# A planned transformer layer: sixteen feed-forward pairs by seven products, six kept results split at once, conditioning sums planned later

## The chip, the cores and the metric

One NeuronCore of a Trainium2 chip runs the kernel. The metric is device microseconds (us) of one execution, median of three runs. TensorE is PE in the profile (its weight loads PEld), VectorE is DVE, ScalarE is ACT, GpSimd is POOL, SyncE is SP; SPq and POOLq are the queues that issue DMAs.

## What is computed

One decoder layer on a 512 x 1024 activation, in float32: a token mixer (attention with 8 heads and a state-space scan with 16 heads, one input and one output projection), then a convolutional gated feed-forward net. A vector c gives shift, scale and gate of both halves through a 1024 x 6144 matrix.

```python
mod = (c_act @ ada_w[i] + ada_b[i])[:, None, :]
sh1, sc1, g1, sh2, sc2, g2 = jnp.split(mod, 6, axis=-1)
h = x * (1.0 + sc1) + sh1
y = hybrid_mixer(h, ...)
x = layer_norm(DEEPNORM_ALPHA * x + (1.0 + g1) * y, ln1_g[i], ln1_b[i])
h = x * (1.0 + sc2) + sh2
y = conv_ffn(h, ...)            # u = causal_dwconv(h @ w_up); (silu(g) * val) @ w_down
x = layer_norm(DEEPNORM_ALPHA * x + (1.0 + g2) * y, ln2_g[i], ln2_b[i])
```

## The kernel before

**Precision.** Each float32 operand is split into a high part (ACT copies it to fp32r) and a low part (DVE subtracts), and every product is three matmuls (high x high, low x high, high x low). So each weight tile costs a load on SP, an ACT copy (`wh`, or half of `wq`) and a DVE subtraction (`wl`, or the other half of `wq`).

**Order of work.** The program is written as generators, one for each chain of work (loads, splits, products, attention of one head pair, and so on). A planner at the head of the file (`Order`) runs them against a table of costs and latencies: at every step it takes, among the heads of all generators, the instruction that can start first by its plan, and among those of one engine that can start within 0.2 us of it the one with the lowest priority number. What it emits is a fixed order for each engine; waits on the chip follow from data. `Region` (L44) holds when a tile's parts are written and read by plan, `try_alloc` (L145) hands out tiles from pools with quotas (`R.limit`), and `start` (L235) works out an instruction's earliest start: written data counts as there after the writer's latency (`LAT`, L231: 1.0 us for a load on SP). Every engine instruction is issued through one helper, L308, so profile rows go by tile names.

**Stages.** First c's shift and scale and the first products; then the input projection (`fm`, `tm`) with attention (`psS` scores, `pT` transposes, `pov`) and the scan beside it; then the output projection (`po`) and the first normalisation (`ln1`, `pt` transposes); then the up projection of the feed-forward net, the *up stage*; last its down projection (`dn`) and the second normalisation.

**Conditioning sums.** `ada_acc` (L1083) loads eight 128 x 1024 pieces of the matrix (tile `ad`, two at a time) and adds each, times a column of c, to `acc` on DVE. `ada_row` and `ada_cols` (L1107, L1120) do that three times during input and output projection, and `ada_last` (L1779) once more, its pieces by two.

**The up stage.** There are 22 pairs of output tiles (gate and value). A pair is done directly (2 tiles x 8 pieces x 3 = 48 matmuls of 512 columns), or, if in `SEVEN` (L694), by seven half-size products as in Strassen's scheme (`seven`, L1660; 7 x 4 x 3 = 84 matmuls of 256 columns, `sP`). Pairs 0 and 1 are done directly in two halves. A seven-product pair needs sums of weight quarters: two are made by accumulating DMAs on POOL (`sums_seven`, L720), two on DVE (`sw`), and seven tiles are split into `wq` (`split_seven`, L763); its products are put together by seven DVE additions of 256 columns (`seven_out`, L1692). Then `up_post` (L1358) does a three-tap convolution on ACT and DVE and multiplies gate by value. The split weights (`wh`/`wl` or `wq`) share a quota `w2` of 11 buffers.

**Kept results.** The product for the down projection must again be split into high and low parts (`mid`). For pairs below `NMID` (4) `up_post` does it at once, in two buffers each. The others are kept unsplit in one tile (`keep`), and the generator `keep` (L1388) splits them once the up stage's tiles are free (mark `fin`), at priority 1. `up_post` runs at priority 2. When kept results 12 to 15 are split, their tiles go to the normalised x, which is loaded back (`x_back`) and scaled on POOL (`row_loads`).

```python
        if j >= NMID:
            ...
            k = KEPT[j] = KEEP[j - j % n][:, j % n]
            yield V.tensor_mul(k, g, u)
            ...
        yield V.tensor_mul(g, g, u)
        mid = yield buf("b", [P, 2, SEQ], "mid", "mid", F32R)
        yield A.activation(mid[:, 0], g, AF.Copy)
        yield V.tensor_sub(mid[:, 1], g, mid[:, 0].bitcast(F32))
```

Of the kernel before, what the change touches and what calls it, by code (L numbers as in the profile page):

```python
# [43 lines left out]
class Region:  # L44


    def __init__(self, base=0.0):
        self.base, self.wr, self.rd, self.psum, self.whole = base, {}, {}, False, False

    def end(self):  # L50
        return max([self.base] + [v[0] for v in self.wr.values()] + [v[0] for v in self.rd.values()])
# [56 lines left out]
class Order:  # L108
# [37 lines left out]
    def try_alloc(self, a):  # L146
        if a.after:
            if self.due(a) > self.time:
                return None
            a.after = ()  # L150
        pool, slots = self.pools[a.cls]
        group = a.group or a.cls
        if self.used.get(group, 0) >= self.quota.get(group, 1000):
            return None
        free = [s for s in slots if s["free"]]
        if not free:
            return None
        s = min(free, key=lambda q: q["end"])
        t = pool.tile(a.shape, a.dt, name=self.name(a.name), tag=s["tag"], bufs=1)
        s["free"] = False  # L160
        self.used[group] = self.used.get(group, 0) + 1
        self.regs[t.tensor.name] = Region(s["end"])
        self.regs[t.tensor.name].psum = a.cls == "ps"
        self.regs[t.tensor.name].whole = a.name == "sP"
        self.owner[t.tensor.name] = (s, group)
        return t

# [71 lines left out]
    def start(self, op, margin=0.0):  # L239
        t = self.clock["G" if op.eng == "GD" else op.eng]  # L240
        for k in op.ins + (op.outs if op.eng == "GD" else []):
            if k:
                r = self.regs[k[0]]
                t = max(t, r.base)
                for c in k[1]:
                    w = r.wr.get(c)
                    assert w or k[0].startswith("dr"), ("read before write", op.fn, k[0], c)
                    if w and w[1] != op.eng:
                        t = max(t, w[0] + self.LAT[w[1]] + margin)
                    elif w:  # L250
                        t = max(t, w[0] + self.SAME[op.eng])
                if r.psum:
                    t = max([t] + [q[0] + 0.12 for q in r.rd.values() if q[1] != op.eng])
        for k in op.outs:
            if k:
                r = self.regs[k[0]]
                t = max(t, r.base)
                for c in k[1]:
                    for w in (r.wr.get(c), r.rd.get(c)):
                        if w and w[1] != op.eng:  # L260
                            t = max(t, w[0] + 0.09 + margin)
        if op.port:
            for a, b in self.held["G" if op.eng == "V" else "V"]:
                if a <= t < b:
                    t = b
        return t
# [146 lines left out]
def layer_kernel(  # L413
# [21 lines left out]
    R = Order(nc)  # L435
    T, V, A, G, S, GD = (Engine(R, k) for k in ("PE", "V", "A", "G", "S", "GD"))
# [26 lines left out]
    def buf(cls, shape, name, group=None, dt=F32):  # L463
        return Alloc(cls, shape, dt, name, group)
# [226 lines left out]
            rows_item(w_out, k, n)  # L691
    UP0 = len(items)
    NSPLIT = 4
    SEVEN = [3, 5, 6, 8, 9, 11, 12, 13, 15, 16, 17, 18, 19, 20, 21]  # L694
    for j, i in up_tiles:
        cols_item(w_up, i * D_FF + j * P)
    for n in range(2):
# [4 lines left out]
    def w_load():  # L702
        yield Need("loads")
        for i, (shape, src) in enumerate(items):
# [4 lines left out]
            j = (i - UP0) // 2  # L709
            if i == UP0 + 2 * j + 1 and j in SEVEN:  # L710
                R.spawn(sums_seven(j, raw, items[i - 1][1][:, :4], src[:, :4]), 4)
# [3 lines left out]
    def sums_seven(j, r1, a11, a21):  # L715

        q = yield buf("s", [P, 4, P], "sw")
        yield S.dma_start(q, a11)
        yield GD.dma_start(r1[:, :4], r1[:, 4:], accum_op=OP.add)
        yield GD.dma_start(q, a21, accum_op=OP.add)  # L720
        QS[j] = q
        R.mark(("qs", j))

    def w_split():
        yield Need(("hk", KC - 1))
        for i, (shape, _) in enumerate(items):
# [6 lines left out]
            if 0 <= i - len(items) + LATE_DN < 2:  # L733
                yield Need("fin")
                m = 2 * (i - len(items) + LATE_DN)
                hi, lo = RES["w"][:, m], RES["w"][:, m + 1]
            elif UP0 <= i < UP0 + 2 * NFF and (i - UP0) // 2 in SEVEN:
                if (i - UP0) % 2 == 0:
# [63 lines left out]
    def w_next():  # L802
        i = wpos[0]
        wpos[0] += 1
        if not (UP0 <= i < UP0 + 2 * NFF and (i - UP0) // 2 in SEVEN):
            lead[0] += 1
# [538 lines left out]


    MID, U, E8 = {}, {}, {}
    NMID = 4
    KEEP, KEPT = {}, {}

    def conv3(ps, dst, ch, neg):
# [6 lines left out]
    def up_post(j, i, ps, neg=False):  # L1358
# [8 lines left out]
        g = U.pop(j)  # L1367
        if j >= NMID:
            if not 12 <= j < 20 and j % 2 == 0:
# [18 lines left out]
    def keep():  # L1388

        yield Need("tsused")  # L1390
        for j in (12, 16):
            KEEP[j] = yield buf("e", [P, 4, SEQ], "keep")
            R.mark(("keep", j))
        yield Need("fin")
        for j in range(NMID, NFF):
            if 12 <= j < 20:
                if j % 2 == 0:
                    E8[j] = yield buf("e", [P, 2, 2, SEQ], "mid2", dt=F32R)
                mid = E8[j - j % 2][:, j % 2]
            else:  # L1400
                mid = yield buf("b", [P, 2, SEQ], "mid", "mid", F32R)
            yield Need(("kept", j))
            yield A.activation(mid[:, 0], KEPT[j], AF.Copy)
            yield V.tensor_sub(mid[:, 1], KEPT[j], mid[:, 0].bitcast(F32))
            MID[j] = mid
            R.mark(("mid", j))
            n = 4 if 12 <= j < 20 else 2
            if j % n == n - 1:
                R.free(KEEP[j - j % n])
                R.mark(("kfree", j - j % n))  # L1410
# [306 lines left out]
    def ffn():  # L1717
        h2h, h2l = H2["hl"]
        pend = []
        for part in range(2):  # L1720
            c0, c1 = part * 256, part * 256 + 256
            for j, i in up_tiles[:NSPLIT]:
                if part == 0:
                    key, n_ = w_next()
                    ps = yield bank("gemm", "up")
                    yield Need(key)
                    w = W.pop(n_)
                    pend.append((ps, w))
                else:
                    ps, w = pend.pop(0)  # L1730
                for k in range(KC):
                    yield Need(("h2", 2 * part, k // 4), ("h2", 2 * part + 1, k // 4))
                    yield mm3(ps[:, c0:c1], w[0][:, k], w[1][:, k], h2h[:, k, c0:c1], h2l[:, k, c0:c1],
                              k == 0, k == KC - 1)
                if part == 1:
                    R.free(*w)
                    R.spawn(up_post(j, i, ps), 2)
        R.free(ROWS.pop("g1p"))
        R.limit(raw=5, w2=11, gemm=8)
        for n, (j, i) in enumerate(up_tiles[NSPLIT:]):  # L1740
            if j in SEVEN:
                if i == 0:
                    yield from seven(j)
                continue
            key, n_ = w_next()
            ps = yield bank("gemm", "up")
            yield Need(key)
            w = W.pop(n_)
            for k in range(KC):
                yield mm3(ps, w[0][:, k], w[1][:, k], h2h[:, k], h2l[:, k], k == 0, k == KC - 1)  # L1750
            R.free(*w)
            R.spawn(up_post(j, i, ps), 2)
        R.free(h2h, h2l, *TS)
        RES["rw"] = yield buf("h", [P, 4, DM], "RW")
        RES["w"] = yield buf("h", [P, 4, 2, 512], "wlast", dt=F32R)
        R.mark("fin")
        R.limit(gemm=8, raw=3, w2=8)
        ps = {}
        cuts = [[(0, 512), (512, DM)]] * 3 + [[(0, 512), (512, 768), (768, DM)]]
        for n in range(2):  # L1760
            for t in range(NT):
                for c in cuts[t][1:] if n else cuts[t][:1]:
                    ps[t, c[0]] = yield bank("gemm", "dn")
                if n == 0:
                    R.spawn(ln2(t, ps, cuts[t]), 0.5 if t == NT - 1 else 1)

            def block(i, tile, w):
                t, (c0, c1) = tile
                s, c = slice(t * P, (t + 1) * P), slice(c0 - n * 512, c1 - n * 512)
                for b in range(2):  # L1770
                    k = 2 * i + b
                    yield Need(("mid", k))
                    yield mm3(ps[t, c0][:, :c1 - c0], MID[k][:, 0, s], MID[k][:, 1, s],
                              w[0][:, b, c], w[1][:, b, c], k == 0, k == NFF - 1)

            tiles = [(t, c) for t in range(NT) for c in (cuts[t][1:] if n else cuts[t][:1])]
            yield from by_tile(tiles, NFF // 2, (1, LATE_DN)[n], block, lambda tile: ("y2", tile[0], tile[1][0]))
# [45 lines left out]
    R.spawn(ada_last(), 8)  # L1823
    R.spawn(quarters(), 1.5)
    R.spawn(x_back(), 6)
    R.spawn(keep(), 1)
    R.run()


# [28 lines left out]
```

## Time and profile before

| | us |
|---|---|
| runs: median (lowest to highest of 3) | 710.2 (709.73 to 711.14) |
| the profiled execution, its own time | 712.51 |
| its span, first to last instruction | 710.8 |
| PE busy in it | 692.5 (97%) |
| DVE busy | 625.9 (88%) |
| ACT busy | 361.1 (51%) |
| POOL busy | 95.5 (13%) |

The profiled execution took 2.3 us more than the median of the runs, and 1.7 us of it lie outside the span. A matmul's span in the trace is longer than its step: the next one begins while it still runs, so PE's rate is read from start to start, and a DVE instruction too begins a little before the end of the one ahead of it. "Idle before" in brackets tells what an engine waited for.

### The profile page before, as it was taken

Reading aid. Unit: us, or ns where it says so; the run is one execution under the profiler, and the core shown is the slowest. Engines: PE = TensorE matmul, PEld = TensorE weight load, DVE = VectorE, ACT = ScalarE, POOL = GpSimd, SP = SyncE. Lnnn points to the kernel's source line nnn. Section 1 sums busy time; section 2 is a strip of 40 time slices with the busy share of each in tenths; the row PEclk is TensorE's granted clock in tenths of the full one; section 3 lists DMA queues with packets and bytes.
Section 4 is the critical chain, followed back from the end, with each engine's and each line's share of the span. In section 5 each row is a group of like instructions: output and inputs, shape, how many; then the busy total and the mean of one; then the engine's idle time right before and its main releaser. Section 6 shows DMA issues by size and latency. Waiting matters only on the chain.

```text
span 710.8 us, 11222 instructions
## 1 busy us (share of the span) xinstructions
PE 692.5 (97%) x4161; PEld 595.5 (84%) x4161; DVE 625.9 (88%) x1169; ACT 361.1 (51%) x662; POOL 95.5 (13%) x101
## 2 busy tenths in 40 slices
PE   8999999999989999999999999999999999999995
PEld 7777878888878788877898898999899998888885
DVE  5879989999988998798999999999999999857645
ACT  3347578746654466233667556465655685211200
POOL 0010021101000000000112020212121104910022
PEclk9999999999999999999999999999999999999998
DMA  9996084044466506876476383957687474332202
GB/s 271 316 289 227 0 243 128 27 116 124 127 194 199 187 30 217 291 257 213 153 180 146 72 196 85 237 122 174 137 189 171 123 260 178 118 98 81 89 30 90
DMA packets 130123, 113.47 MB, mean 160 GB/s; under 512 B 4373, under 2 KB 109201, under 8 KB 130067
## 3 DMA queue, kind: packets, MB, share of 16 engines
q1 hardware_dynamic: 119987, 104.88, 48.0%
q0 software_dynamic: 10080, 7.87, 7.8%
q8 instruction: 33, 0.54, 0.3%
q14 instruction: 23, 0.19, 0.1%
HBM read 104.56 MB, written 4.23 MB: 153 GB/s over the span
## 4 chain that ended last, share of the span: by engine, by line
PE 79%; DVE 7%; DMA 6%; SPq 4%; issue 2%; ACT 1%; POOL 0%; DVEq 0%; ACTq 0%; POOLq 0%
PE sP L308 18%; PE dn L308 17%; PE fm L308 15%; PE up L308 9%; PE po L308 6%; SPq L308 4%; PE tm L308 2%; DMA ad<-in_ada_w_dram 2%; PE first L308 2%; PE pov L308 1%; PE pT L308 1%; PE psS L308 1%; DVE u L308 1%; PE py L308 1%; DVE wl L308 1%
## 5 line engine op out<-in xcount | busy, mean ns | idle before, releaser
L308 DVE TENSOR_TENSOR wl<-raw,wh 128x1024 fp32r<-128x1024 f32 x72 | 92.4, 1289 | 21.2 <-ACT wh L308 20.9
L308 ACT ACTIVATE wh<-raw 128x1024 fp32r<-128x1024 f32 x72 | 75.3, 1055 | 70.0 <-DVE raw L308 23.3
L308 PE MATMUL dn<-wh,mid 128*128 128x512 f32 (+1 forms) x356 | 102.9, 372 | 0.0
L308 PE MATMUL sP<-ts,wq 128*128 128x256 f32 x720 | 90.2, 281 | 0.0
L308 PEld LDWEIGHTS sP<-ts,wq 128*128 128x128 f32 x720 | 87.5, 189 | 0.0
L308 PEld LDWEIGHTS dn<-wh,mid 128*128 128x128 f32 x356 | 64.6, 188 | 12.7
L308 PE MATMUL fm<-hh,wh 128*128 128x512 f32 x176 | 72.9, 414 | 0.0
L308 PE MATMUL sP<-h2h,wq 128*128 128x256 f32 x360 | 69.8, 282 | 0.7 <-DVE sP L308 0.7
L308 PE MATMUL fm<-hl,wh 128*128 128x512 f32 x176 | 69.8, 396 | 0.0
L308 PE MATMUL fm<-hh,wl 128*128 128x512 f32 x176 | 69.7, 396 | 0.0
L308 PE MATMUL dn<-wl,mid 128*128 128x512 f32 (+1 forms) x178 | 66.1, 371 | 0.0
L308 PEld LDWEIGHTS sP<-h2h,wq 128*128 128x128 f32 x360 | 57.7, 189 | 1.3 <-DVE sP L308 1.1
L308 PE MATMUL sP<-h2l,wq 128*128 128x256 f32 x180 | 50.5, 281 | 0.0
L308 PE MATMUL up<-h2h,wh 128*128 128x512 f32 (+1 forms) x144 | 49.6, 344 | 0.0
L308 PE MATMUL up<-h2h,wl 128*128 128x512 f32 (+1 forms) x144 | 49.4, 343 | 0.0
L308 PE MATMUL up<-h2l,wh 128*128 128x512 f32 (+1 forms) x144 | 49.4, 343 | 0.0
L308 PE MATMUL po<-wh,os 128*128 128x512 f32 x128 | 42.9, 398 | 0.0
L308 DVE SCALAR_TENSOR_TENSOR acc<-ad,csil,acc 128x1024 f32<-128x1024 f32 x28 | 35.8, 1282 | 6.2 <-DMA ad<-in_ada_w_dram 5.9
L308 DVE TENSOR_TENSOR wq<-raw,wq 128x512 fp32r<-128x512 f32 x60 | 40.5, 685 | 0.6 <-ACT wq L308 0.5
L308 PEld LDWEIGHTS fm<-hh,wl 128*128 128x128 f32 x176 | 33.3, 189 | 7.8
L308 PEld LDWEIGHTS fm<-hh,wh 128*128 128x128 f32 x176 | 33.4, 190 | 7.2 <-ACT Y L308 0.4
L308 PEld LDWEIGHTS dn<-wl,mid 128*128 128x128 f32 x178 | 33.5, 188 | 6.3
(269 smaller groups left out, 1539.0 us busy)
## 6 DMA issues: line engine op xcount, KB each, us to landing
raw<-in_ffn_up_w_dram SPq DMA_DIRECT2D x44, 512.0 KB
raw<-in_mix_in_w_dram SPq DMA_DIRECT2D x26, 512.0 KB
ad<-in_ada_w_dram SPq DMA_DIRECT2D x24, 512.0 KB
raw<-in_ffn_down_w_dram SPq DMA_DIRECT2D x22, 512.0 KB
aw<-in_ada_w_dram SPq DMA_DIRECT2D x32, 256.0 KB
raw<-in_mix_out_w_dram SPq DMA_DIRECT2D x12, 512.0 KB
csb<-drcs SPq DMA_DIRECT2D x8, 512.0 KB
ad<-in_ada_w_dram SPq DMA_DIRECT2D x4, 1024.0 KB
```

The source lines that it names most:

```text
L308: getattr(self.hw[op.eng], op.fn)(*op.args, **op.kw)
```

## The change

Five edits:

- Pairs 7 and 10 are done by seven products, and pair 9 directly: 16 pairs in place of 15, in runs 5 to 8 and 10 to 13 where runs 5 to 6, 8 to 9 and 11 to 13 stood.
- `NMID` is 6: results 4 and 5 are split at once.
- `w2` is 10 in the up stage.
- `keep` has priority 2.5, behind `up_post`.
- The planner counts data of `ad` tiles that SP loads as there 2.0 us later than before (3.0 us after the load's planned end). This is a figure of the plan alone; no wait is added to the program.

```diff
-        self.base, self.wr, self.rd, self.psum, self.whole = base, {}, {}, False, False
+        self.base, self.wr, self.rd, self.psum, self.whole, self.late = base, {}, {}, False, False, 0.0
...
+        self.regs[t.tensor.name].late = 2.0 if a.name == "ad" else 0.0
...
                     if w and w[1] != op.eng:
-                        t = max(t, w[0] + self.LAT[w[1]] + margin)
+                        t = max(t, w[0] + self.LAT[w[1]] + margin + (r.late if w[1] == "S" else 0.0))
...
-    SEVEN = [3, 5, 6, 8, 9, 11, 12, 13, 15, 16, 17, 18, 19, 20, 21]
+    SEVEN = [3, 5, 6, 7, 8, 10, 11, 12, 13, 15, 16, 17, 18, 19, 20, 21]
...
-    NMID = 4
+    NMID = 6
...
-        R.limit(raw=5, w2=11, gemm=8)
+        R.limit(raw=5, w2=10, gemm=8)
...
-    R.spawn(keep(), 1)
+    R.spawn(keep(), 2.5)
```

The planner makes another order of it from the second half of the input projection on. Three places follow (the new file's helper line is L309).

DVE in the input projection, beside the attention of head pair 1 (`pr_1972`: its last softmax rows; `psS`, read by the ISA rows: scores of head pair 2). Before:

```order
L308 SCALAR_TENSOR_TENSOR acc_804<-ad_2137,csil_75,acc_804 128x1024
L308 SCALAR_TENSOR_TENSOR qk_2132<-fm_2074,qs_83,qk_2132 64x512
L308 RECIPROCAL mx_2051<-mx_2051 128x1
L308 TENSOR_SCALAR pr_1972<-pr_1972,mx_2051 128x512
L308 ISA pr_2116,mx_2143<-psS_2118,M_84 128x128
L308 ISA mx_2143 128x1
L308 SCALAR_TENSOR_TENSOR acc_804<-ad_2164,csil_75,acc_804 128x1024
L308 TENSOR_TENSOR wl_2195<-raw_1866,wh_2194 128x1024
L308 TENSOR_SCALAR mx_2143<-mx_2143 128x1
L308 ISA pr_2116,mx_2210<-psS_2119,M_84 128x128
```

Now:

```order
L309 SCALAR_TENSOR_TENSOR acc_804<-ad_2126,csil_75,acc_804 128x1024
L309 SCALAR_TENSOR_TENSOR qk_2132<-fm_2074,qs_83,qk_2132 64x512
L309 RECIPROCAL mx_2051<-mx_2051 128x1
L309 TENSOR_SCALAR pr_1972<-pr_1972,mx_2051 128x512
L309 ISA pr_2116,mx_2140<-psS_2118,M_84 128x128
L309 ISA mx_2140 128x1
L309 TENSOR_SCALAR mx_2140<-mx_2140 128x1
L309 ISA pr_2116,mx_2179<-psS_2119,M_84 128x128
L309 ISA mx_2179 128x1
```

Between the two ISA rows on `psS_2118` and `psS_2119` stood a conditioning sum and a weight split; now only the sign change of a maximum stands there. The next two sums come 20 and 31 rows after the first row shown, and one sum fewer stands ahead of `pr_1972`.

PE at the transposes of `pr_1972`. Before, six matmuls into the following projection tile:

```order
L308 MATMUL fm_2192<-hh_95,wl_1945 128x512
L308 MATMUL pT_2182<-ident_68,pr_1972 128x128 x4
L308 MATMUL pT_2213<-ident_68,pr_1972 128x128 x4
L308 MATMUL fm_2192<-hh_95,wh_1944 128x512
L308 MATMUL fm_2192<-hl_96,wh_1944 128x512
```

Now:

```order
L309 MATMUL fm_2131<-hh_95,wl_1853 128x512
L309 MATMUL pT_2177<-ident_68,pr_1972 128x128 x4
L309 MATMUL pT_2182<-ident_68,pr_1972 128x128 x4
L309 MATMUL fm_2131<-hh_95,wh_1852 128x512
L309 MATMUL fm_2131<-hl_96,wh_1852 128x512
```

The transposes stand twelve 512-column matmuls earlier: after the eighteenth matmul of `fm_2131`, where they stood after all its 24 and six of the next tile.

DVE after the last weight split of the up stage (`wq_6180` before, `wq_6252` now), up to the first split of a kept result. Before, all that stands there:

```order
L308 TENSOR_TENSOR wq_6180<-sw_6129,wq_6180 128x512
L308 TENSOR_TENSOR sP_6125<-sP_6125,u_1187_6091 128x256
L308 TENSOR_TENSOR sP_6125<-u_1187_6091,m_1178_6045 128x256
L308 TENSOR_TENSOR wl_6200<-raw_5927,wh_6199 128x1024
L308 TENSOR_TENSOR sP_6107<-sP_6107,u_1187_6091 128x256
L308 SCALAR_TENSOR_TENSOR u_6054<-sP_5972,fprm_90,u_6054 128x511
L308 SCALAR_TENSOR_TENSOR u_6054<-sP_5972,fprm_90,u_6054 128x510
L308 TENSOR_TENSOR u_1206_6222<-sP_6160,m_1198_6178 128x256
L308 TENSOR_TENSOR keep_4485<-u_6054,u_6041 128x512
L308 TENSOR_TENSOR wl_6225<-raw_6069,wh_6224 128x1024
L308 TENSOR_TENSOR wl_6282<-raw_6071,wh_6281 128x1024
L308 TENSOR_TENSOR mid_6301<-keep_4151,mid_6301 128x512
```

(one more row like the eighth is left out). Now, the last of 32 instructions ahead of it:

```order
L309 SCALAR_TENSOR_TENSOR u_6314<-sP_6192,nfw_92,u_6314 128x510
L309 SCALAR_TENSOR_TENSOR u_6319<-sP_6173,fprm_90,u_6319 128x511
L309 SCALAR_TENSOR_TENSOR u_6319<-sP_6173,fprm_90,u_6319 128x510
L309 SCALAR_TENSOR_TENSOR u_6418<-sP_6331,nfw_92,u_6418 128x511
L309 SCALAR_TENSOR_TENSOR u_6418<-sP_6331,nfw_92,u_6418 128x510
L309 TENSOR_TENSOR keep_6455<-u_6319,u_6314 128x512
L309 SCALAR_TENSOR_TENSOR u_6420<-sP_6312,fprm_90,u_6420 128x511
L309 TENSOR_TENSOR wl_6432<-raw_6273,wh_6431 128x1024
L309 SCALAR_TENSOR_TENSOR u_6420<-sP_6312,fprm_90,u_6420 128x510
L309 TENSOR_TENSOR mid_6368<-keep_4507,mid_6368 128x512
```

The 32 are 13 additions of 256 columns, 12 convolution taps, 5 weight splits of 1024 columns and 2 products; the first kept result is number 6 where it was 4.

## Rows read from the trace of the kernel before

**Rows 1.** The page's part 1, the engines' busy time over the span.

```profile
PE 692.5 (97%) x4161; PEld 595.5 (84%) x4161; DVE 625.9 (88%) x1169; ACT 361.1 (51%) x662; POOL 95.5 (13%) x101
```

**Rows 2.** The waits of PE by releaser: us in total, times, longest us.

```profile
PE pT L308 <- DVE mx L308: 2.4, 1, 2.4
PE pt L308 <- DVE XN L308: 1.0, 1, 1.0
PE sP L308 <- DVE sP L308: 0.7, 2, 0.4
```

**Rows 3.** Timeline of PE, 206 to 214 us: start us, us, instructions, idle before.

```profile
206.79 0.60 PE L308 MATMUL pT<-ident,pr 128*128 128x128 f32 x4
209.84 1.02 PE L308 MATMUL pT<-ident,pr 128*128 128x128 f32 x4 [2.45 <-DVE mx L308]
211.09 0.63 PE L308 MATMUL fm<-hl,wh 128*128 128x512 f32 x1
211.52 0.63 PE L308 MATMUL fm<-hh,wl 128*128 128x512 f32 x1
213.77 0.40 PE L308 MATMUL fm<-hh,wh 128*128 128x512 f32 x1
```

**Rows 4.** Busy time by stretch: window, length, PE, PEld, DVE, ACT, POOL, PEclk, DMA share, GB/s.

```profile
210.00:220.00 10.00, 10.00 (x60) 8.22 (x60) 8.45 (x27) 6.02 (x15) 0.00 (x0) 0.83 0.48 154
```

**Rows 5.** Timeline of DVE, 204 to 210 us.

```profile
204.35 0.49 DVE L308 TENSOR_SCALAR pr<-pr,mx 128x512 f32<-128x512 f32 x1
207.10 1.28 DVE L308 SCALAR_TENSOR_TENSOR acc<-ad,csil,acc 128x1024 f32<-128x1024 f32 x1 [1.93 <-DMA ad<-in_ada_w_dram]
208.30 1.22 DVE L308 TENSOR_TENSOR wl<-raw,wh 128x1024 fp32r<-128x1024 f32 x1
209.43 0.15 DVE L308 TENSOR_SCALAR mx<-mx 128x1 f32<-128x1 f32 x1
209.49 0.28 DVE L308 CUSTOM_DVE_ANT_0 pr<-psS,M 128x128 f32<-128x128 f32 x1
```

**Rows 6.** Timeline of DVE in the first normalisation, 336 us.

```profile
335.90 1.28 DVE L308 SCALAR_TENSOR_TENSOR acc<-ad,csil,acc 128x1024 f32<-128x1024 f32 x1 [1.11 <-DMA ad<-in_ada_w_dram]
```

**Rows 7.** The chain that ended last, three pieces: start us, us, what.

```profile
458.16 11.11 PE up L308 x48
510.25 69.56 PE sP L308 x588
579.81 123.06 PE dn L308 x594
```

**Rows 8.** Groups of DVE instructions, shapes apart.

```profile
L308 DVE TENSOR_TENSOR wl<-raw,wh 128x1024 fp32r<-128x1024 f32 x72 | 92.4, 1289 | 21.2 <-ACT wh L308 20.9
L308 DVE TENSOR_TENSOR wq<-raw,wq 128x512 fp32r<-128x512 f32 x60 | 40.5, 685 | 0.6 <-ACT wq L308 0.5
L308 DVE SCALAR_TENSOR_TENSOR u<-sP,fprm,u 128x510 f32<-128x510 f32 x15 | 11.2, 749 | 0.5
```

**Rows 9.** Busy time by stretch: the up stage, and early in the down stage.

```profile
360.00:580.00 220.00, 219.12 (x1612) 207.59 (x1611) 213.83 (x372) 132.79 (x227) 30.77 (x28) 1.00 0.67 156
600.00:624.00 24.00, 24.00 (x105) 19.37 (x104) 20.71 (x14) 5.93 (x7) 23.45 (x14) 1.00 0.37 123
```

**Rows 10.** Timeline of DVE around the end of the up stage.

```profile
569.88 0.69 DVE L308 TENSOR_TENSOR wq<-raw,wq 128x512 fp32r<-128x512 f32 x1
570.48 0.42 DVE L308 TENSOR_TENSOR u<-sP,m 128x256 f32<-128x256 f32 x1
570.81 0.69 DVE L308 TENSOR_TENSOR wq<-raw,wq 128x512 fp32r<-128x512 f32 x1
572.41 0.69 DVE L308 TENSOR_TENSOR wq<-sw,wq 128x512 fp32r<-128x512 f32 x1
...
598.50 1.60 DVE L308 TENSOR_TENSOR keep<-u,u 128x512 f32<-128x512 f32 x1
604.88 1.77 DVE L308 TENSOR_TENSOR mid<-keep,mid 128x512 fp32r<-128x512 f32 x1
```

## The prediction

> **What bounds the kernel now.** I read the engines' totals first, then the waits of PE, then the timelines around each wait, and the chain that ended last for the rates.
>
> PE is busy for 692.5 of 710.8 us [rows 1], so what it does not do is little, and the change can win in two ways only: fewer matmul steps, or less of the waits. The reader should see in the totals that VectorE (DVE) stands at 88% over the whole span, and then that this average hides the up stage: from 360 to 580 us DVE is busy for 213.83 of 220 us [rows 9]. There two engines are nearly full at once.
>
> The waits of PE name one long one: 2.45 us on DVE's `mx`, beside 1.0 us in the first normalisation and 0.7 us for the put-together sums `sP` [rows 2]. The long one is at 207 to 210 us, ahead of the second four transposes of `pr` [rows 3]. It costs more than its length: in the window from 210 us the granted clock is 0.83 [rows 4], and the two matmuls at 211.09 and 211.52 stand 0.43 us apart, at half rate (1.2 GHz), where 594 matmuls of the down stage take 123.06 us, among them transposes, and 48 direct ones 11.11 us, 0.231 us each [rows 3, 7]. From the transposes' start at 209.84 to the matmul at 213.77 go 3.93 us; the same instructions at full rate would take 2.29 us (the eight products between them at 0.231 and the transposes 0.44). So the wait costs 2.45 + 1.64 = 4.1 us.
>
> What made it is on DVE: the conditioning sum `acc` stood 1.93 us idle for its load, took 1.20, and a weight split took 1.13 more [rows 5]. Only then came the read of the scores `psS` at 209.49 [rows 5], whose bank the transposes needed. In the first normalisation the same shows again: `acc` waits 1.11 us for `ad` [rows 6].
>
> **The change part by part.**
>
> *One more pair by seven products.* A direct pair is 11.11 us, a seven-product pair 84 of 588 matmuls in 69.56 us, that is 9.94 us [rows 7]. Three pairs change kind, net one: **-1.2 us**. This is sure, since PE issues fewer columns, unless the time comes back as a wait.
>
> *What VectorE pays for it.* From start to start a 128x512 two-input operation takes 0.60 us and a 256-column addition 0.33 [rows 10]; a weight split of 1024 columns 1.13 [rows 5]. The pair adds seven splits and two sums of 0.60 and seven additions of 0.33, and saves two splits of 1.13: 5.4 + 2.3 - 2.3 = 5.4 us. Two more kept results split at once add 2 x 0.60. So DVE has 6.6 us more in the up stage, and that stage is 1.2 us shorter: 7.8 us less room. In the trace the room is 6.2 us of idle time over 220 us [rows 9], and a lead at the end: the last `wq` split begins at 572.41 and ends by 573.0 [rows 10], its twelve matmuls begin 1.42 us ahead of the down stage's 579.81 [rows 7], so at 578.4, 5.4 us later. The lead that is left, L, is thus between 5.4 - 7.8 = -2.4 us (no idle time is taken) and 5.4 + 6.2 - 7.8 = +3.8 us (all of it). Where it is below nothing, PE has waited for it.
>
> *The down stage's start.* Behind that last split DVE now has the 32 instructions of the third place above before the first kept result is split: 13 additions at 0.33, 12 taps at 0.67 (their 0.749 us [rows 8] less the 0.08 by which the next begins early), five splits at 1.13, two products at 0.60: 19.2 us, and 20.4 with the splits of results 6 and 7. The six split at once carry three steps of 24 matmuls, 16.65 us, and the stage starts 1.42 us + L after the split. So results 6 and 7 come 20.4 - 18.1 - L = 2.3 - L us late. With the waits of the up stage that is nothing at L over 2.3 and 4.7 us at L = -2.4. I take the middle of the bounds, L = 0.7: **+1.6 us**. Before, only 4 to 5 us of such work stood behind the kept splits' mark; the new priority puts it ahead of them.
>
> *The conditioning sums.* At the first place no sum and no split stands any more between the two reads of `psS`. The transposes of `pr` come twelve matmuls (2.8 us) earlier on PE, near 204.0 us, and DVE, without the sum that now comes later (1.20 us), has `pr` at 204.84 - 1.2 = 203.6 [rows 5]; the two reads and the small rows between them (0.28 us and less each) bring it to about 204.5, where PE, after four transposes, wants the bank at 204.45. The wait of 4.1 us goes; late next is that same read, by nothing to 0.5 us, and I take 0.3: **-3.8 us**. The cover for a late load is then the 20 and 31 rows that stand ahead of the next sums. In the first normalisation the 1.11 us for `ad` goes, but a third sum (1.20 us) stands between the first and third row tile: between -1.3 (both the wait and its trailing 0.3) and +0.2; **-0.6 us**, the middle. If a load is late there all the same, the cost is what it is now.
>
> *Fewer buffers, queues.* A seven-product tile is held for 12 matmuls, 1.42 us, so ten buffers still allow a lead of 14 us, over the 5.4 us there was: nothing, and at most one tile's 1.42 us where DVE would have been further ahead. POOL issues two more accumulating loads; its share of the up stage is 30.77 of 220 us [rows 9], and the sums are needed pairs later: nothing. SP issues the `ad` loads later; the load itself is not longer, and DMA's share there is 0.48 [rows 4]: nothing, unless a weight load now stands behind them, which is the first rival.
>
> The sum: -1.2 - 3.8 - 0.6 + 1.6 = -4.0 us, so the profiled execution would go from 712.5 to 708.5. That execution stood 2.3 us over the median of the runs, so the median goes from 710.2 to **706.2 us**.
>
> *A rule that speaks against it.* Kept splits that come later come beside POOL's scaling of x. Of 24 us from 600 us POOL is busy for 23.45 [rows 9], and there a kept split takes 1.77 us and a kept product 1.60, where the same shape took 0.69 at 570 us [rows 10]. POOL can't start before results 12 to 15 are split, which leaves six, in three steps: two splits and two weight splits take 2 x 1.77 + 2 x 1.13 = 5.8 us, against 5.55 of PE, so 0.25 us a step if DVE has no lead. Result 16 is due eight steps, 44 us, into the stage, so I count nothing. The Trainium skill, page "SBUF — State Buffer", section "Who interferes with whom", says that a VectorE operation with two SBUF inputs contends with a GpSimd operation that reads SBUF, and that the one which issued second stands still for the whole of the other. By that, every further split moved behind POOL's start costs its 1.1 us again. The rows agree on the size, but can't tell whether it is the port.
>
> **The rivals.**
>
> *A: the wait moves within the attention.* The planner rewrote everything from 194 us on, and four sums now stand close together ahead of `pr`; any of them can wait for its load as the one at 207.10 did for 1.93 us [rows 5]. For it: in both places where a sum waits today it is the load [rows 5, 6]. Against: the loads are planned 2 us later than before, about that wait. A wait of the old size gives 706.2 - 0.3 + 4.1 = 710.0 us: no change.
>
> *B: VectorE becomes the bound at the end of the up stage.* The mechanism is the sum above at its worst end, L = -2.4, with waits of 4.7 us at the last splits and at the start of the down stage, each followed by half clock as at 210 us (1.64 each): 8.0 us. Without any such wait the median would be 710.2 - 1.2 - 3.8 - 0.6 = 704.6, so this gives 712.6 us, slower. It decides from 7.0 us of waits and half clock on. For it: 213.83 of 220 us are taken [rows 9], and little idle time can be moved to the right place. Against: PE waited only 0.7 us for `sP` in the whole kernel [rows 2], and never for a split there.
>
> *C: kept splits beside POOL.* By the 0.25 us a step, over three steps 0.8 us, over all eight 2.0: 707.0 to 708.2 us, still faster.
>
> **How the numbers follow.** The forecast has 0.54, C 0.10, A 0.17 and B 0.19. Runs of this kernel lie 1.4 us apart, 0.2%, which is about what a measurement can tell from no change. Forecast and C are faster than 708.8 us: 0.64; A is within 0.2%: 0.17; B is slower: 0.19. The best end is 1.2 + 4.1 + 1.3 = 6.6 us, so 703.6, and the lowest run lies 0.5 us under its median: the range starts at 703.0. Upward it takes in A and the milder half of B: 712.0. What is left out is about a tenth at the upper side and little below.
>
> **What would show it.** Right: no wait of `pT` over 0.5 us near 204 us and a granted clock of 1.00 from 200 to 220; no `acc` on DVE idle over 0.5 us for `ad`; seven-product runs at 9.94 us a pair; PE's first wait of the down stage at results 6 and 7, 16.65 us after its start, of some 1.6 us in all. Wrong: a PE wait on `wq` or `sP` over 1 us between 360 and 580 us, with a clock under 1.00 behind it (B); a wait of 2 us anywhere from 194 to 350 us (A); kept splits over 1.6 us with PE waiting for `mid` later than 44 us into the stage (C).

## The result, and the profile after

| | before | the change |
|---|---|---|
| runs, first chip: median (lowest to highest) | 710.29 (709.73 to 711.14) | 706.97 (706.36 to 707.25) |
| ratio, with its 95% interval | | 0.9946 (0.9933 to 0.9959) |
| the profiled execution, its own time (span) | 712.51 (710.8) | 707.04 (705.3) |
| the same kernel again, another chip | 710.59 (709.68 to 712.53) | 706.30 (705.89 to 706.99), ratio 0.9943 (0.9927 to 0.9959) |

Faster by 3.3 us on the first chip and by 4.3 on the second; forecast were 4.0. The two profiled executions stand 5.5 us apart, since the one of before was 2.3 us over its median and the one of the change is within 0.1 of its own. Part 1 of the page of the change, which answers to [rows 1]:

```profile
PE 690.0 (98%) x4197; PEld 596.6 (85%) x4197; DVE 623.6 (88%) x1182; ACT 362.7 (51%) x670; POOL 99.5 (14%) x103
```

The waits of PE by releaser behind the program's start (us in total, times, longest us), which answer to [rows 2], and PE and the stretches around the place of [rows 3, 4] (columns as there):

```profile
PE pt L309 <- DVE XN L309: 0.9, 3, 0.4
PE pad L309 <- DVE accl L309: 0.7, 1, 0.7
PE sP L309 <- ACT m L309: 0.5, 1, 0.5
```

```profile
205.16 1.09 PE L309 MATMUL pT<-ident,pr 128*128 128x128 f32 x8
206.00 0.48 PE L309 MATMUL fm<-hh,wh 128*128 128x512 f32 x1
```

```profile
200.00:210.00 10.00, 10.00 (x75) 8.35 (x74) 9.63 (x25) 5.63 (x13) 1.04 (x2) 1.00 0.50 144
210.00:220.00 10.00, 9.98 (x56) 7.74 (x55) 9.44 (x24) 7.76 (x20) 0.00 (x0) 1.00 0.43 131
```

The wait on `mx` is not in the list any more, and behind the start, the same in both programs, none over 0.7 us in one piece has come in its place. The eight transposes of `pr` run in one piece from 205.16 us, the next matmul follows 0.84 us later, and the granted clock is 1.00 from 200 to 220 us where it was 0.83. The first normalisation still costs PE 0.9 us, now in three pieces. VectorE at the same place, answering to [rows 5]:

```profile
202.41 1.28 DVE L309 SCALAR_TENSOR_TENSOR acc<-ad,csil,acc 128x1024 f32<-128x1024 f32 x1
...
204.72 0.49 DVE L309 TENSOR_SCALAR pr<-pr,mx 128x512 f32<-128x512 f32 x1
205.23 0.29 DVE L309 CUSTOM_DVE_ANT_0 pr<-psS,M 128x128 f32<-128x128 f32 x1
...
205.64 0.28 DVE L309 CUSTOM_DVE_ANT_0 pr<-psS,M 128x128 f32<-128x128 f32 x1
...
207.75 1.28 DVE L309 SCALAR_TENSOR_TENSOR acc<-ad,csil,acc 128x1024 f32<-128x1024 f32 x1
```

Neither sum, at 202.41 or at 207.75 us, waited, and 0.41 us lie between the two reads of the scores at 205.23 and 205.64, where there were 4.6 (204.86 to 209.49). Among VectorE's waits `ad` is gone; before it stood there with 5.9 us in seven waits:

```profile
DVE acc L308 <- DMA ad<-in_ada_w_dram: 5.9, 7, 1.9
```

The end of the chain, the stretches that answer to [rows 9], and VectorE's timeline around the last weight split (columns as in [rows 7, 9, 10]):

```profile
505.33 69.64 PE sP L309 x588
574.97 122.93 PE dn L309 x594
```

```profile
360.00:580.00 220.00, 218.66 (x1636) 208.48 (x1635) 216.57 (x386) 134.12 (x234) 32.47 (x30) 1.00 0.67 158
600.00:624.00 24.00, 24.00 (x105) 19.41 (x104) 13.48 (x9) 4.77 (x5) 23.45 (x14) 1.00 0.46 148
```

```profile
567.51 0.69 DVE L309 TENSOR_TENSOR wq<-sw,wq 128x512 fp32r<-128x512 f32 x1
...
588.06 1.28 DVE L309 TENSOR_TENSOR mid<-keep,mid 128x512 fp32r<-128x512 f32 x2
...
603.31 0.96 DVE L309 TENSOR_TENSOR mid<-keep,mid 128x512 fp32r<-128x512 f32 x1 [2.13 <-ACT mid L309]
```

Seven pairs take 69.64 us, 9.95 each. The last split `wq` ends 0.60 us after its start, at 568.1; its matmuls begin 1.42 us ahead of 574.97, so at 573.55: a lead of 5.4 us, as long as before the change. Results 6 and 7 are split from 588.06 to 589.3 us, and PE needs them 16.65 us after 574.97, at 591.6: 2.3 us early, not late. No wait stands in the down stage.

### The profile page after: what moved, and what is told of

Read it like the earlier page. It is cut to its first block, busy times and chain, and to the rows that moved or that the text cites. A ratio compares the mean times of both kernels' runs of the same rounds, so it can differ in the third digit from the quotient of the medians.

```text
span 705.3 us, 11343 instructions
## 1 busy us (share of the span) xinstructions
PE 690.0 (98%) x4197; PEld 596.6 (85%) x4197; DVE 623.6 (88%) x1182; ACT 362.7 (51%) x670; POOL 99.5 (14%) x103
## 4 chain that ended last, share of the span: by engine, by line
PE 83%; DVE 9%; DMA 3%; SPq 2%; issue 1%; ACT 1%; POOL 0%; DVEq 0%; POOLq 0%; ACTq 0%
PE sP L309 22%; PE fm L309 17%; PE dn L309 17%; PE po L309 6%; PE up L309 5%; PE first L309 4%; SPq L309 2%; PE tm L309 2%; PE psS L309 2%; PE pov L309 1%; PE pT L309 1%; DVE u L309 1%; PE py L309 1%; DMA wr<-in_mix_in_w_dram 1%; DMA csb<-drcs 1%
## 5 line engine op out<-in xcount | busy, mean ns | idle before, releaser
L309 DVE TENSOR_TENSOR wl<-raw,wh 128x1024 fp32r<-128x1024 f32 x70 | 88.0, 1260 | 25.8 <-ACT wh L309 25.6
L309 ACT ACTIVATE wh<-raw 128x1024 fp32r<-128x1024 f32 x70 | 73.5, 1054 | 68.8 <-DVE raw L309 23.3
L309 PE MATMUL dn<-wh,mid 128*128 128x512 f32 (+1 forms) x356 | 102.8, 371 | 0.0
L309 PE MATMUL sP<-ts,wq 128*128 128x256 f32 x768 | 96.4, 281 | 0.5 <-ACT m L309 0.5
L309 PEld LDWEIGHTS sP<-ts,wq 128*128 128x128 f32 x768 | 93.2, 188 | 0.8 <-ACT m L309 0.7
L309 PEld LDWEIGHTS dn<-wh,mid 128*128 128x128 f32 x356 | 64.5, 188 | 12.7
L309 PE MATMUL sP<-h2h,wq 128*128 128x256 f32 x384 | 74.2, 281 | 0.0
L309 PE MATMUL fm<-hh,wh 128*128 128x512 f32 x176 | 72.5, 412 | 0.0
L309 PE MATMUL fm<-hh,wl 128*128 128x512 f32 x176 | 69.3, 394 | 0.0
L309 PE MATMUL fm<-hl,wh 128*128 128x512 f32 x176 | 69.3, 394 | 0.0
L309 PE MATMUL dn<-wl,mid 128*128 128x512 f32 (+1 forms) x178 | 66.0, 371 | 0.0
L309 PEld LDWEIGHTS sP<-h2h,wq 128*128 128x128 f32 x384 | 61.5, 189 | 0.2
L309 PE MATMUL sP<-h2l,wq 128*128 128x256 f32 x192 | 53.9, 281 | 0.0
L309 PE MATMUL up<-h2h,wh 128*128 128x256 f32 (+1 forms) x128 | 43.2, 338 | 0.0
L309 PE MATMUL up<-h2l,wh 128*128 128x256 f32 (+1 forms) x128 | 43.2, 337 | 0.0
L309 PE MATMUL up<-h2h,wl 128*128 128x256 f32 (+1 forms) x128 | 43.2, 337 | 0.0
L309 DVE TENSOR_TENSOR wq<-raw,wq 128x512 fp32r<-128x512 f32 x64 | 42.9, 684 | 0.1
L309 PE MATMUL po<-wh,os 128*128 128x512 f32 x128 | 42.1, 396 | 0.0
L309 PEld LDWEIGHTS fm<-hh,wl 128*128 128x128 f32 x176 | 33.0, 188 | 7.7
L309 PEld LDWEIGHTS fm<-hh,wh 128*128 128x128 f32 x176 | 33.2, 188 | 7.1 <-issue 0.7
L309 ACT ACTIVATE wq<-raw 128x512 fp32r<-128x512 f32 x64 | 37.4, 622 | 3.1 <-PE sP L309 2.8
L309 PEld LDWEIGHTS dn<-wl,mid 128*128 128x128 f32 x178 | 33.4, 188 | 6.3
```

What stands on the lines that cost most here:

```text
L309: getattr(self.hw[op.eng], op.fn)(*op.args, **op.kw)
```

## The experiments

Every kernel here was timed beside the kernel before on its chip. Since the chips differ and the start of the program (the same in all, some 105 us) takes up to 1.7 us more or less from one profile to the next, the table has one more column: the stretch of the profiled execution from PE's first matmul of the scan's `py`, near 106 us, to its first of `dn`, read off PE's timelines. The runs from before_again to no_late were on one chip, those from no_late_no_load to keep_first on another, the last four on a third; the first profiles of before and of the change come from the chip of the result.

| kernel | median | ratio to before (95%) | stretch py to dn |
|---|---|---|---|
| before, first profile | 710.2 | | 473.7 |
| before_again | one run, 710.08 | | 471.1 |
| sums_no_load | 706.32 | 0.9939 (0.9919 to 0.9958) | 467.7 |
| late_only | 707.38 | 0.9957 (0.9941 to 0.9972) | 468.8 |
| no_late | 713.02 | 1.0035 (1.0017 to 1.0052) | 474.9 |
| no_late_no_load | 708.48 | 0.9969 (0.9952 to 0.9986) | 470.9 |
| pairs_15 | 709.25 | 0.9979 (0.9965 to 0.9993) | 470.1 |
| pairs_17 | 712.38 | 1.0023 (1.0010 to 1.0037) | 473.8 |
| keep_first | 708.08 | 0.9965 (0.9947 to 0.9982) | 467.7 |
| the change, first profile | 706.97 | 0.9946 (0.9933 to 0.9959) | 467.7 |
| after_again | 706.30 | 0.9943 (0.9927 to 0.9959) | 467.6 |
| late_only_again | 707.76 | 0.9960 (0.9945 to 0.9975) | 469.1 |
| w2_11 | 706.75 | 0.9949 (0.9933 to 0.9964) | 467.8 |
| spread_16 | 707.37 | 0.9957 (0.9941 to 0.9973) | 468.9 |

**1. before_again: is the wait always the same?** No edit.

> The kernel before, unchanged, profiled a second time. The profiled execution before stood 2.3 us over the median of the runs, and the medians differ by 3.3 us where the profiles differ by 5.5. Theory (the wait for a conditioning load is not the same length in each execution): PE's wait for mx near 207 us is shorter here by 0.5 us or more, and the execution's own time is nearer to 710.3 us. Rival (the surplus lies elsewhere): the wait is 2.2 to 2.7 us again with the granted clock at 0.83 behind it, and the time differs in another place.

The timelines of VectorE and PE in this second profile of the kernel before:

```profile
200.38 1.28 DVE L308 SCALAR_TENSOR_TENSOR acc<-ad,csil,acc 128x1024 f32<-128x1024 f32 x1 [1.54 <-DMA ad<-in_ada_w_dram]
...
206.63 1.28 DVE L308 SCALAR_TENSOR_TENSOR acc<-ad,csil,acc 128x1024 f32<-128x1024 f32 x1
```

```profile
206.76 0.50 PE L308 MATMUL fm<-hh,wh 128*128 128x512 f32 x1 [1.10 <-DVE mx L308]
...
209.37 0.66 PE L308 MATMUL pT<-ident,pr 128*128 128x128 f32 x4 [0.51 <-DVE mx L308]
```

```profile
210.00:220.00 10.00, 9.95 (x66) 7.69 (x65) 9.44 (x28) 6.99 (x18) 0.00 (x0) 1.00 0.52 156
```

Here another sum waited, the one at 200.38 us, for 1.54 us, and the load that was late in the first profile was there in time at 206.63. PE waited 1.10 and 0.51 us in place of 2.45, and the clock stayed at 1.00. So the 4.1 us that the first profile showed is one outcome among several: here the same fault took 1.6 us, and the stretch is 2.6 us shorter. This holds with the theory, and the difference between the profiles (5.5) and the medians (3.3) can be in it.

**2. sums_no_load: the same order, no load to wait for.** The instruction order is that of before on all engines; the 28 sums read `acc` in place of the piece, which leaves that part of the modulation out.

```diff
-        getattr(self.hw[op.eng], op.fn)(*op.args, **op.kw)
+        getattr(self.hw[op.eng], op.fn)(*(op.args[:1] * 2 + op.args[2:] if op.eng == "V" and op.fn == "scalar_tensor_tensor" and op.args[1].tensor.name.startswith("ad_") else op.args), **op.kw)
```

> The kernel before in its own order on every engine, but the 28 conditioning sums that add a loaded piece read their own accumulator in its place: no sum waits for a load (the output is left without those parts of the modulation; the loads themselves are still made). Load theory: no wait of PE for mx over 0.5 us between 200 and 215 us, granted clock 1.00 there, no idle time of VectorE on ad; 2.0 to 4.8 us less than before, so 705.5 to 708.3. Rival (VectorE's order makes the wait, with its sum and weight split between the two reads of the scores): the wait stays within 0.6 us of its length, and the time within 1.0 us of before.

```profile
208.08 0.66 PE L308 MATMUL pT<-ident,pr 128*128 128x128 f32 x4 [0.24 <-DVE mx L308]
```

On PE's timeline the wait is 0.24 us, and VectorE's idle time on `ad` is 0.2 us. The time falls by 4.4 us. Load theory; with VectorE's order as it was, sum and weight split between the two reads included, the rival is refuted. One thing more changes in this run: a piece's tile comes free without its sum (SP's queue waits 10.7 us for `acc` where it waited 22.1), and what earlier loads add to the 4.4 us was not separated.

**3. late_only and no_late: the two halves of the change.** In the first, the later planning is added to the kernel before (the first three pieces of the diff shown ahead of the prediction, nothing else). In the second, it is taken out of the changed kernel:

```diff
-        self.regs[t.tensor.name].late = 2.0 if a.name == "ad" else 0.0
+        self.regs[t.tensor.name].late = 0.0 if a.name == "ad" else 0.0
```

> The kernel before with the later planning of the conditioning loads (2.0 us) alone. VectorE's order is the changed kernel's up to the end of the conditioning sums, and its own behind. Load theory: the part of the gain that does not come from the pair is here, 710.3 less 2.0 to 3.6, so 706.7 to 708.3, and PE shows no wait over 0.5 us from 194 to 225 us. Rival (the gain comes from the up stage and the start of the down stage): within 1.0 us of before.

> The changed kernel without the later planning: pair, kept results, buffers and priority only. Load theory: 0.5 to 2.0 us less than before (the pair's 1.2 us), so 708.3 to 709.8, with VectorE idle for ad over 3 us in sum and a wait of PE near 207 us as before. Rival: over 2.3 us less than before, below 708.0.

The planning alone gives 3.3 us. The rest of the change alone does not give 0.5 to 2.0 us, it costs 2.3: in time both expectations for no_late missed. The waits that the theory named are there (5.2 us of VectorE on `ad`, 1.48 us of PE at 207.17), but another one stands beside them. PE and VectorE in its profile, and the stretch:

```profile
554.07 2.50 PE L309 MATMUL sP<-ts,wq 128*128 128x256 f32 x10 [2.77 <-DVE wq L309]
```

```profile
549.95 1.53 DVE L309 SCALAR_TENSOR_TENSOR u<-sP,nfw,u 128x511 f32<-128x511 f32 x2 [0.29 <-ACT u L309]
551.40 1.28 DVE L309 TENSOR_TENSOR keep<-u,u 128x512 f32<-128x512 f32 x2
552.72 0.69 DVE L309 TENSOR_TENSOR sw<-sw,raw 128x512 f32<-128x512 f32 x1
553.33 0.69 DVE L309 TENSOR_TENSOR wq<-sw,wq 128x512 fp32r<-128x512 f32 x1
```

```profile
550.00:560.00 10.00, 7.23 (x49) 7.03 (x48) 9.93 (x17) 6.40 (x12) 2.16 (x2) 0.83 0.62 166
```

PE waits 2.77 us for a split `wq` at 554 us. VectorE is not idle there: it takes two taps, two kept products and a sum `sw` first. The granted clock is 0.83 in the mean of the 10 us: the next ten matmuls span 2.50 us, where twelve span 1.59 at 558.30, at full rate again. That is the mechanism of rival B, though 20 us earlier than I put it.

**4. no_late_no_load: does the idle time travel?** The substitution of run 2, in the order of no_late.

> The changed kernel without the later planning, in its own order, with the 28 conditioning sums reading their own accumulator in place of the loaded piece (that part of the modulation is left out). In that order with the loads PE waited 2.9 us for a split wq at 551 us, 200 us after the last sum. Theory one (VectorE's 5.2 us of idle time for ad is carried on as a backlog to the end of the up stage): that wait falls below 0.5 us, and the kernel lies 5.5 us or more under 713.0, at 707.5 or less. Theory two (the order of that stretch makes the wait, whatever came before): the wait stays at 2.0 us or more; the kernel gains the 3.0 to 4.5 us of the attention alone, 708.5 to 710.0.

```profile
549.82 1.64 PE L309 MATMUL sP<-ts,wq 128*128 128x256 f32 x10 [2.77 <-DVE wq L309]
```

The wait of 2.77 us for `wq` is there again (PE's timeline), so theory two holds: the order of that stretch makes it, not time that VectorE lost 200 us before. The kernel gains 0.9969 against 1.0035, 4.7 us, a little over the theory's 4.5 and about what the loads are worth in run 2. What the later planning does for the up stage thus lies in the order that the planner then finds; room on VectorE alone doesn't take this wait away.

**5. pairs_15 and pairs_17: one pair fewer, one more.**

```diff
-    SEVEN = [3, 5, 6, 7, 8, 10, 11, 12, 13, 15, 16, 17, 18, 19, 20, 21]
+    SEVEN = [3, 5, 6, 8, 9, 11, 12, 13, 15, 16, 17, 18, 19, 20, 21]
```

```diff
-    SEVEN = [3, 5, 6, 7, 8, 10, 11, 12, 13, 15, 16, 17, 18, 19, 20, 21]
+    SEVEN = [3, 5, 6, 7, 8, 10, 11, 12, 13, 14, 15, 16, 17, 18, 19, 20, 21]
```

> The changed kernel with the 15 seven-product pairs of before; kept results, buffers, priority and later planning as changed. Theory (the sixteenth pair is worth its PE time, since VectorE keeps its lead): 0.8 to 1.6 us slower than the changed kernel, 707.7 to 708.6, no wait of PE over 1 us from 360 to 600 us. Rival (VectorE's added work gives the pair back): within 0.5 us of the changed kernel, 706.4 to 707.5.

> The changed kernel with pair 14 by seven products too, 17 pairs. It adds 5.4 us to VectorE and takes 1.2 us from PE, 6.6 us less room, where the changed kernel shows a lead of 5.4 us at the last split and 3.4 us of idle time from 360 to 580 us. Theory (room is what decides, and a lead of 2.2 us or less is too little): waits of PE on VectorE of 1 us or more from 360 to 600 us, and 706.0 to 709.5. Rival (the lead is not used up, as it was not by the sixteenth): no such wait, 705.2 to 706.2.

With 15 pairs the kernel is 2.3 us slower than the change by the ratios, so the theory's 0.8 to 1.6 is missed, and the rival too. The stretch is 2.5 us longer, more than the pair: one more wait stands in it, 0.98 us on ACT, from PE's timeline:

```profile
509.38 2.83 PE L309 MATMUL sP<-ts,wq 128*128 128x256 f32 x22 [0.98 <-ACT m L309]
```

So this run doesn't measure the pair cleanly; late_only_again, below, does. With 17 the rival falls: PE waits for VectorE's `u` once a pair, four times in a row and 5.2 us in all, and the kernel is slower than before. The theory has the waits right, but not their price: it gave 709.5 us at most. One of the waits, and one pair's stretch of this kernel and of the changed one:

```profile
535.20 0.36 PE L309 MATMUL sP<-h2h,wq 128*128 128x256 f32 x1 [1.27 <-DVE u L309]
```

```profile
534.40:545.70 11.30, 10.04 (x84) 9.88 (x84) 11.20 (x21) 6.40 (x13) 2.18 (x2) 1.00 0.70 147
```

```profile
535.10:545.10 10.00, 10.00 (x86) 9.95 (x84) 9.96 (x22) 6.32 (x12) 2.16 (x2) 1.00 0.90 192
```

In the 17-pair kernel this pair takes 11.30 us (the four of the run 11.3 to 11.7) of which VectorE is busy 11.20; PE could do it in 9.94. That is VectorE's own price of a seven-product pair when nothing can be put off any more. The changed kernel, in the same place, moves on at PE's rate with VectorE at 9.96 of 10.00: the rest of what a pair costs was done ahead or is left behind. The granted clock is 1.00 through these waits.

The theory's measure of room, the lead of the last split, doesn't show the difference. In the 17-pair kernel the last `wq` split and the stage's last `ts` matmuls, ahead of the twelve that need it, are:

```profile
572.59 0.69 DVE L309 TENSOR_TENSOR wq<-sw,wq 128x512 fp32r<-128x512 f32 x1
```

```profile
576.73 1.57 PE L309 MATMUL sP<-ts,wq 128*128 128x256 f32 x12
```

The split ends at 573.2 and the twelve begin at 578.1, 4.9 us later, in a kernel that has just waited four times for VectorE. Read in the same way off the timelines the lead is 5.2 us before and 5.3 in the change, and 6.6 in no_late, where PE waited 2.77.

**6. keep_first: the kept results as before.**

```diff
-    NMID = 6
+    NMID = 4
...
-    R.spawn(keep(), 2.5)
+    R.spawn(keep(), 1)
```

> The changed kernel with four results split at once and the kept ones at priority 1, as before. Theory (the later kept splits matter: they leave VectorE to the last sums): a wait of PE on VectorE of 1 us or more between 540 and 600 us, 0.7 to 4 us slower than the changed kernel, 707.7 to 711.0. Rival (they are hidden either way, since result 6 came 2.3 us ahead of its use): within 0.5 us of it, 706.4 to 707.5.

The stretch to `dn` is that of the changed kernel, 467.7 us; PE then waits 0.49 us for VectorE's `u` on its way to the first kept result:

```profile
576.95 0.50 PE L309 MATMUL dn<-wh,mid 128*128 128x512 f32 x1 [0.49 <-DVE u L309]
```

From the first `py` to the end it is 0.7 us longer than the change (598.8 against 598.2). By the ratios it is 1.3 us slower, and the intervals overlap (from 0.9947 to 0.9959). So the theory's time, 0.7 to 4 us, may hold, while the wait of 1 us or more that it named did not come; the rival's 0.5 us is under both figures. Neither is shown.

**7. after_again, late_only_again, w2_11, spread_16: on one chip.** The change; late_only; and the change with

```diff
-        R.limit(raw=5, w2=10, gemm=8)
+        R.limit(raw=5, w2=11, gemm=8)
```

or with

```diff
-    SEVEN = [3, 5, 6, 7, 8, 10, 11, 12, 13, 15, 16, 17, 18, 19, 20, 21]
+    SEVEN = [3, 4, 5, 7, 8, 9, 11, 12, 13, 14, 16, 17, 18, 19, 20, 21]
```

> The changed kernel again, on the chip of the next three, so that they are compared with it. 0.9946 of before as the first time, within 0.002; the wait for the scores near 207 us absent again, lead and kept splits as in its first trace.

> The later planning alone, beside the changed kernel on one chip. Theory (with the lead kept, the pair is worth its PE time, 1.2 us): 0.6 to 1.8 us slower than the changed kernel. Rival (the pair and the rest of the change bring nothing on their own): within 0.5 us of it.

> The changed kernel with 11 buffers for split weights in place of 10. VectorE's order differs in a dozen rows. Theory (a lead of 5.4 us is well under the 14 us that ten buffers allow): within 0.5 us of the changed kernel, the last split ends 5 to 6 us ahead of its matmuls. Rival (the buffers limit the lead at the first seven-product run): 0.5 us or more faster, with a larger lead.

> The changed kernel with its six direct pairs at 0, 1, 2, 6, 10 and 15, in place of 0, 1, 2, 4, 9 and 14: the last run of seven-product pairs is six long, not seven. In the 17-pair kernel VectorE needed 11.3 to 11.7 us a seven-product pair in the long run where PE needs 9.94, so a run eats the lead by 1.3 to 1.8 us a pair and a direct pair gives it back. Theory (the lead of the changed kernel is enough for its longest run): the same time within 0.5 us. Rival (the runs' lengths decide): over 0.5 us faster, with PE's waits for sP under 0.3 us.

The change is confirmed. Late_only is 1.5 us slower than it (1.1 in the first pair of profiles, by the stretch), as the theory said. It lacks the other edits too, and part of the difference lies ahead of the up stage, where the orders are the same. From PE's first matmul of the up projection to its first of `dn` both profiles of late_only take 232.3 us and both of the change 231.4, as do keep_first and w2_11: the pair gives 0.9 us there, of the 1.2 that its products save. Eleven buffers make no difference that can be told (0.45 us the other way, lead 5.3 us): the theory. Other places for the direct pairs make none in their favour, 1.1 us slower: the rival falls, and the theory's 0.5 us is missed too; 0.4 us of the longer stretch lies behind the first matmul of the up projection, where PE has one more short wait for `sP`, the other 0.9 us ahead of it, where the two orders are the same (there the two profiles of late_only differ by 0.4 us). No kernel that computes the whole layer beats the change.

## Why the prediction was right, point by point

The median was forecast at 706.2 us and came at 706.97, and 706.30 on the second chip. Two of its terms were off, the first normalisation and the end of the up stage, and they cancelled by luck. Luck too is the step from the profile to the median: it took a gain of 4.0 us, priced in one execution, off the median, and the profiles then differed by 5.5.

*The pair, -1.2 us.* About right: 9.95 us a pair, and 0.9 us between late_only and the change in the up stage. (The 594 matmuls of the down stage that the prediction sets beside it hold no transposes but 132 products of 256 columns; no term rests on them.) "Unless the time comes back as a wait" is what no_late and pairs_17 show.

*The conditioning sums, -3.8 and -0.6 us.* The mechanism is right: runs 2 and 3, and the profile after. What the waits for the loads cost in the kernel before is right too, 4.4 us by run 2, but not as I put it together: "costs 2.45 + 1.64 = 4.1 us" is one execution, and the next profile of the same kernel lost 1.6 us at this place. The later planning brings 2.8 to 3.3 of the 4.4 (late_only); the term that was mis-sized is the first normalisation, "-0.6 us, the middle". The wait for `ad` [rows 6] went, and the third sum and other work of VectorE took its place. The waits of PE from there on in late_only, and the one that is left of them in sums_no_load:

```profile
PE pt L309 <- DVE XN L309: 0.9, 3, 0.4
PE pad L309 <- DVE accl L309: 0.7, 1, 0.7
PE sP L309 <- ACT m L309: 0.5, 1, 0.5
```

```profile
PE sP L308 <- DVE sP L308: 0.3, 1, 0.3
...
PE pad L308 <- DVE accl L308: 0.2, 1, 0.2
```

That is 2.1 us against 0.5, so of the 4.4 us some 1.6 go into small waits at the normalisation, at the last row of the modulation (`pad`) and at the first run of seven-product pairs; by the medians, and by the stretch, late_only is 1.1 us behind sums_no_load. At the normalisation itself the waits were 1.0 us before [rows 2] and are 0.9 now, so of the term's 0.6 us 0.1 came, and the 0.5 us more at `pad` had no term. The new wait of 0.3 us near 204 us did not come.

*VectorE at the end of the up stage, +1.6 us.* Wrong: nothing. The step that failed is L, "between -2.4 and +3.8 us"; it was 5.4. It was to be what is left of VectorE's room, and it is not: about 5 us stand there in the kernel before, in the change and in the 17-pair kernel, which has no room. And I took all of VectorE's work before the last split as fixed but for what the edit adds. The stretches from the third normalised tile to the end of the last split, before and after:

```profile
346.50:573.00 226.50, 225.50 (x1662) 213.41 (x1661) 220.43 (x386) 136.54 (x235) 34.08 (x31) 1.00 0.68 158
```

```profile
343.60:568.10 224.50, 222.99 (x1692) 213.50 (x1692) 220.99 (x392) 139.64 (x246) 35.76 (x33) 1.00 0.69 162
```

VectorE's busy time grew by 0.6 us there, not by 6.6. The instructions that begin in the two stretches show most of the rest. Three `hk` and one `XN` of the normalisation (1.5 us from start to start) went from VectorE to ScalarE. The `hk` in these stretches, before and after:

```profile
L308 DVE TENSOR_SCALAR hk<-pt,mcol 128x128 f32<-128x128 f32 x9 | 3.1, 405 | 0.0
```

```profile
L308 ACT ACTIVATE hk<-pt,mcol 128x128 f32<-128x128 f32 x7 | 3.0, 456 | 2.5 <-PE pt L308 2.2 <-DVE hk L308 0.3
```

```profile
L309 DVE TENSOR_SCALAR hk<-pt,mcol 128x128 f32<-128x128 f32 x6 | 2.3, 404 | 0.0
```

```profile
L309 ACT ACTIVATE hk<-pt,mcol 128x128 f32<-128x128 f32 x10 | 3.9, 448 | 0.3 <-DVE hk L309 0.3
```

One `h2l` (0.6 us) was done ahead of the stretch, and two taps and three additions (2.3 us) more are left behind the last split. Idle time gave another 2.6 us (6.07 to 3.51). No_late shows that this outcome hung on the order that the planner found: with the same pairs and the other order PE waited 2.77 us.

*Work behind the last split, 20.4 us.* About right: results 6 and 7 were split 21.2 us after it. With L = 5.4 that is early.

*Kept splits beside POOL.* Most did not move behind its start, they moved ahead of it: at 597.9 us POOL begins, 12 of 16 are split by then, three follow at once at their short length, and the last, at 603.31, takes 0.96 us. The groups of kept splits and kept products, after; before they were 18 each at 808 and 800 ns:

```profile
L309 DVE TENSOR_TENSOR keep<-u,u 128x512 f32<-128x512 f32 x16 | 11.0, 686 | 0.0
...
L309 DVE TENSOR_TENSOR mid<-keep,mid 128x512 fp32r<-128x512 f32 x16 | 10.3, 702 | 2.1 <-ACT mid L309 2.1
```

So rival C had no ground here. The Trainium skill, page "SBUF — State Buffer", section "Who interferes with whom", would have predicted the long forms beside POOL; the trace agrees that one of the two is long where they meet. POOL's first two additions:

```profile
597.90 4.43 POOL L309 TENSOR_TENSOR XN<-XN,l 128x512 f32<-128x512 f32 x1 [46.62 <-DMA XN<-drxn]
```

```profile
602.41 1.31 POOL L309 TENSOR_TENSOR XN<-XN,l 128x512 f32<-128x512 f32 x1
```

The first took 4.43 us while VectorE ran three kept splits and, at 599.96, a weight split of 1.22 us, all short; the second, most of it with VectorE idle, took 1.31. Later it is VectorE that is long: a weight split takes 2.15 us at 604.36. No run here shows that the port is what they meet in.

*The rivals.* A did not come: no wait over 0.6 us from 194 to 350 us. B did not come in the change, but VectorE is the bound one step away, in no_late (1.0035), with the half clock that B has, and in pairs_17 (1.0023), without it; the change sits between two orders that lose. The 0.19 for it was not too much.

*Left open.* Why the planner's order for the up stage is good with the later planning and bad without it was not traced back to one choice. One part is on record: the later planning alone moves the three `hk` and the `XN` to ScalarE (they are there in late_only, and not in no_late). A wait from the load side alone, with the order of no_late made good by hand, was not tried.

## What to carry to other kernels

Before a wait is priced from one trace, look how that execution stands to the median: a wait for a load moves between neighbouring instructions from run to run, and what it costs moves with it. Where the second engine is as full as the first, its idle time is no bound on what it can still take: work is moved ahead of the stretch, behind it and to a third engine, and what decides is whether the order puts the needed split ahead of work that can wait. The price to compare is the one per unit in a long run (11.3 to 11.7 us a pair for VectorE, 9.94 for PE): work done ahead or left behind pays the difference, and in the 17-pair kernel it no longer did. A lead read at the end of the run does not tell how much of that is left.

## What the runs showed of the hardware

A wait of PE of 2.45 us [rows 3] and two of 2.77 us were each followed by a stretch of 0.83 granted clock over 10 us, with matmuls at half rate; waits of 1.48 us, of 1.10 and 0.51 us close together, and of 1.15 to 1.46 us once every 11.5 us were followed by none: the clock stayed at 1.00. The first of the long ones cost 1.64 us beside its length; what the short ones cost beside theirs was not worked out.
